# Moving the conditioning of a hybrid decoder step partly into its feed-forward stage, and changing three places of the hand-written order

## The chip, the core and the metric

The kernel is one program on one core of a Trainium2 chip. Its time is the device time in microseconds (us) of one execution of the program, inputs and outputs in the chip's memory. The core has a matrix engine (TensorE, PE in the profile), three engines for elementwise work (VectorE or DVE, ScalarE or ACT, GpSimd or POOL), and SyncE (SP), whose queue issues most of the DMA transfers here. PE works on operands in SBUF and writes to PSUM, from which VectorE and ScalarE read.

## What is computed

Two layers of a decoder, for 512 prompt positions and 8 samples of 4 positions, 544 columns in all, with 1024 features:

```
mod = (silu(c) @ w_ada + b_ada).reshape(B, 6, 1, D_MODEL)     # six sections
h = rmsnorm(x, norm1_g) * (1 + mod[:, 1]) + mod[:, 0]
z = h @ w_in
... four mixers on column ranges of z: pooling, retention, short convolution, RWKV-7
mixed = sum(sigmoid(gates) * (branches @ w_br)) @ w_out
x = x + mod[:, 2] * mixed
h2 = rmsnorm(x, norm2_g) * (1 + mod[:, 4]) + mod[:, 3]
up = causal_dwconv(h2 @ w_up);  act = silu(up[:D_FF]) * up[D_FF:]
x = x + mod[:, 5] * (act @ w_down)
```

After the second layer comes a final norm. The states of the mixers and of the convolution are outputs too. All matrices are float32.

So each of the six sections of the conditioning `mod` has a place at which it must be there: 0 and 1 at a layer's start, 2 at the residual after the mixers, 3 and 4 at the second norm, and 5 at the residual of the down projection. Layer 1's sections depend on `c` alone and can be computed at any time before.

## The kernel before, in words

**Layout and weights.** Activations lie with features on the 128 partitions and the 544 columns along the free dimension, in two halves of 272 (`HS`). The large matrices are cut into "units" of eight 128 x 128 tiles (0.5 MB), 138 per layer, in the order in which they are used. `load_unit` (L100) brings a unit in through a buffer `raw` (three of them), ScalarE casts it to a high part (L109), VectorE (GpSimd for two units) subtracts to get a low part (L110). `mm3` (L125) then takes three matmuls per tile: high x high, high x low, low x high (L129, L130, L131). A unit's products with all 544 columns are thus 48 matmuls. `getw(l, u, ahead)` issues loads up to unit `u + ahead`. There are four buffers for a unit's high and low parts; `extra_pools` can give a unit other buffers, among them a large tile of the pool `T4` (14 tiles of 2176 floats per partition).

**Order.** PE's order is the order of the program text. The other engines and SP's queue are ordered by a planner when the program is built, which can place an instruction earlier than its place in the text. Side work is written as generators that `slot` (L154) advances, called after each `mm3`: a generator yields how many main matmuls must pass before its next step (`yield 30`); a negative number makes a step that needs no PE slot, `True` marks a "tiled" step, that is one with many small matmuls. A generator with a slack (`spawn(..., 60)`) waits for such a tiled step, or until it is 60 matmuls late while another generator is due, or 240 otherwise. `finish(e)` runs all remaining steps of a generator at once.

**Conditioning.** Sections 0 and 1 of layer 0 are computed at the start. `ada` (L216) computes other sections: eight slices of weights are loaded, one after the other (0.5 MB each for one section, 1 MB for two sections at once), each is multiplied in four PE column groups (L225), the result is copied (L231), transposed back (L235) and added to the bias. It pauses at the start of each section (`yield 60`), between slices (`yield 30 * ns`) and before the transposes (`yield 18`). Layer 0's sections 2 to 5 run as `ada0` with slack 60 beside the mixers, through the same `raw` buffers as the weights; `finish(ada0)` (in the layer's loop, after the last gate) ends them before the output projection. Layer 1's six sections run in pairs as `ada_next` beside layer 0's up projection, through `T4` tiles.

**Norms by halves.** `both_halves` (L311) runs a projection first for the columns of one half, then of the other; while the second half is projected, the first is normalised (`norm_half`, L292). The second half is normalised while the next projection runs on the first: four units at the start of layer 1 (`for i in range(4)`), and four units, the first two pairs (`up_pairs([0, 1], True)`), at the start of each feed-forward stage.

**RWKV.** `rwkv` (L383) prepares 32-step blocks, inverts a 32 x 32 triangular matrix for each block and head by a substitution on VectorE (`substitute`, L558 and L560), writes the inverses to memory (`scr2`) and reads them back block by block into a diagonal tile `XT`, which has to be zero elsewhere (L569). Then 16 chunks follow one another: per chunk a matmul L639, copies by ScalarE and VectorE (`g_out`, L601), a matmul L606 after `D_G` = 12 main matmuls, copies (`sa_of`, L610), after `D_S` = 12 more the matmuls L659 and L663, VectorE's update of the state (L671, L677), and after `D_P` = 18 the next chunk. At the same time the main stream runs the other mixers; the pooling branch (two units) ends each of them with a series of VectorE additions and scalings (L1133 to L1152).

**Feed-forward.** `up_pairs` and `down` alternate: ten pairs, `down(0)`, four pairs, `down(1)`, eight pairs, `down(2)`, `down(3)`. The results of two pairs share one `T4` tile (`acts`), which lives until the `down` that uses it is over.

Of the kernel before, what the change touches and what calls it, by code (L numbers as in the profile page):

```python
# [11 lines left out]
F32R = mybir.dt.float32r  # L12
# [31 lines left out]
def tile_hybrid_step(ctx: ExitStack, tc: tile.TileContext, io: dict):  # L44
    nc = tc.nc
    V, S, G, PE = nc.vector, nc.scalar, nc.gpsimd, nc.tensor
    L = io["wst"].shape[0]
# [50 lines left out]
    extra_pools = {}  # L98

# [116 lines left out]
    def ada(l, sec, ns, load):  # L216

        W = 256 * ns
        ps = PM()
        raws = [load(k) for k in range(ns)]  # L220
        yield 60
        for k in range(0, 8, ns):
            for i in range(ns):
                for n in range(4):
                    PE.matmul(ps[32 * n:32 * n + 32, 0:W], lhsT=sc[:, k + i, :], rhs=raws[k + i][:, W * n:W * n + W],  # L225
                              start=(k + i == 0), stop=(k + i == 7))
            if k + ns < 8:
                raws.extend(load(k + ns + i) for i in range(ns))
                yield 30 * ns
        sb = ZR(W)  # L230
        S.copy(sb, ps[:, 0:W])  # L231
        yield 18
        pt = PM()
        for q in range(2 * ns):
            PE.transpose(pt[:, q * 128:(q + 1) * 128], sb[:, q * 128:(q + 1) * 128], ident)  # L235
        V.tensor_tensor(
            out=mods[l][:, 8 * sec:8 * sec + 8 * ns, :].rearrange("p (n q) j -> p n q j", q=2 * ns),
            in0=pt[:, 0:W].rearrange("p (q n j) -> p n q j", q=2 * ns, n=4)[:, :, :, 0:9],
            in1=pars[l][:, P_BADA + 8 * sec:P_BADA + 8 * sec + 8 * ns].rearrange("p (n q) -> p n q", q=2 * ns).unsqueeze(3)
            .broadcast_to([128, 4, 2 * ns, 9]), op=ADD)  # L240
        scales(l, range(sec, sec + ns), slice(0, 8))

    def ada_load(l, sec, ns):
        def f(k):
            if ns == 1:
                t = wp.tile([128, 1024], F32, tag="raw", name=nm("raw"), bufs=3)
            else:
                t = T4(w=(2176,))[:, 0:2048]
            nc.sync.dma_start(t.rearrange("p (s n) -> p s n", s=ns), io["wada"][l, sec:sec + ns, k].rearrange("s p n -> p s n"))
            return t  # L250
        return f

    def ada_all(l, secs, ns):
        for q in secs[::ns]:
            yield from ada(l, q, ns, ada_load(l, q, ns))
# [127 lines left out]
    def rwkv(l, za, zb, M, yD):  # L383
# [157 lines left out]
        nc.sync.dma_start(X, io["xinit"])  # L541
        yield 24
# [24 lines left out]

        XT = T4(w=(17, 128))
        G.memset(XT, 0.0)  # L569
# [5 lines left out]
        yield 48  # L575
# [360 lines left out]
    for l in range(L):  # L936
# [61 lines left out]
        else:  # L998
            ws = [getw(l, u) for u in range(4)]
            for half in range(2):  # L1000
                for i in range(4):
                    evac_rw(i, unit(ws[i], 0, hops, half), half)
                finish(ng)
            nfirst = 4
# [7 lines left out]
        if l == 0:  # L1012
            ada0 = spawn(ada_all(0, range(2, 6), 1), -30, 60)
# [196 lines left out]
        def extra(i):  # L1210
            def f():
                if i < 2:
                    return (wop.tile([128, 1024], F32R, name=nm("woh")), wop.tile([128, 1024], F32R, name=nm("wol")))
                t = T4(F32R, w=(2176,))
                return t[:, 0:1024], t[:, 1024:2048]
            return f
        for i in range(4):
            extra_pools[(l, ui + 4 + i)] = extra(i)
# [24 lines left out]
        if l + 1 < L:  # L1243
            ada_next = spawn(ada_all(l + 1, range(6), 2), -60)
# [73 lines left out]
        up_pairs([0, 1], True)  # L1318
        up_pairs(range(2, 10))
# [8 lines left out]
        for i in range(4, FFN_PARTS[3][1] - FFN_PARTS[3][0]):  # L1328
            extra_pools[(l, ui + i)] = extra(2)
# [215 lines left out]
```

## Time and profile before

| | |
|---|---|
| median of 3 runs | 1988.12 us (1980.52, 1988.12, 1989.43) |
| the profiled execution | 1981.39 us, its span 1979.3 us |
| granted TensorE clock, mean | 0.991 |
| PE busy | 1908.6 us, 96% |
| VectorE, ScalarE, GpSimd busy | 1111.1, 822.2, 322.6 us |
| HBM read, written | 213.33 MB, 9.06 MB |

The profile's times are those of one execution, in us from its first instruction. A row of a group reads: line, engine, operation, output <- inputs, then the count and the durations; "idle before <- releaser" is what an engine waited for. A row of the waits reads: who <- for whom: total, times, longest. A row of the windows gives the stretch, its width, the busy time of PE, of the weight loads, of VectorE, ScalarE and GpSimd, each with the number of instructions, then the granted clock, the DMA engines' share and GB/s; where it is asked for one source line, only PE's columns stand. A row of the timeline reads: start, duration, engine, line, operation, shapes, count, and the idle time before it with its cause. A row of the DMA issues gives count, size and the median time to landing.

### The profile page before, as it was taken

The numbers are of one execution on the slowest core, as the hardware profiler recorded it, in microseconds if no ns is written. First come the engines' busy times: TensorE is split into PE (matmuls) and PEld (weight loads), VectorE is DVE, ScalarE is ACT, GpSimd is POOL, SyncE is SP. The second block draws the span as 40 slices with busy tenths as digits, with TensorE's granted clock in tenths as the row PEclk, the third lists the DMA queues.
The fourth block names the chain that finished last, engine by engine and source line by source line (L and its number), as shares of the span: only waits on it lengthen the run. The fifth ranks groups of instructions, "written<-read, shape, count | busy, mean of one in ns | idle before, by whom it ended". The sixth has DMA issues, their size and how long they took to land. (4 is left out here: it accounts for less than half of the span.)

```text
span 1979.3 us, 39216 instructions
## 1 busy us (share of the span) xinstructions
PE 1908.6 (96%) x16188; PEld 1831.9 (93%) x16188; DVE 1111.1 (56%) x2267; ACT 822.2 (42%) x1574; POOL 322.6 (16%) x627
## 2 busy tenths in 40 slices
PE   5999899999999999999999998999999999999997
PEld 4999889899988889999999998899999999999997
DVE  5476655643457454556664766555435666455565
ACT  4642333452345442435446432335424565243542
POOL 2120123213001110112202201232120022011210
PEclk9999999999989999999999999999999999999999
DMA  7334234433446752222332132134224132222231
GB/s 310 97 100 125 90 99 139 154 108 97 140 158 241 269 203 96 86 86 86 114 125 87 57 105 68 44 100 132 76 97 163 51 97 93 90 86 86 88 102 46
DMA packets 75555, 227.15 MB, mean 115 GB/s; under 512 B 20209, under 2 KB 23073, under 8 KB 73585
## 3 DMA queue, kind: packets, MB, share of 16 engines
q1 hardware_dynamic: 69872, 210.43, 31.7%
q0 software_dynamic: 3536, 11.53, 1.7%
q10 hardware_dynamic: 1968, 2.69, 0.5%
q8 instruction: 127, 2.08, 0.4%
q14 instruction: 52, 0.42, 0.1%
HBM read 213.33 MB, written 9.06 MB: 112 GB/s over the span
## 5 line engine op out<-in xcount | busy, mean ns | idle before, releaser
L129 PE MATMUL pd<-t,whi 128*128 128x272 f32 x4200 | 1235.9, 294 | 8.5 <-DVE zr L337 3.7
L131 PE MATMUL pd<-t,wlo 128*128 128x272 f32 x4200 | 1216.3, 290 | 0.0
L130 PE MATMUL pd<-t,whi 128*128 128x272 f32 x4200 | 1210.5, 288 | 0.9 <-DVE t L381 0.7
L129 PEld LDWEIGHTS pd<-t,whi 128*128 128x128 f32 x4200 | 792.8, 189 | 40.3 <-issue 26.7
L130 PEld LDWEIGHTS pd<-t,whi 128*128 128x128 f32 x4200 | 794.7, 189 | 2.7 <-DVE t L381 1.8
L131 PEld LDWEIGHTS pd<-t,wlo 128*128 128x128 f32 x4200 | 793.4, 189 | 0.0
L110 DVE TENSOR_TENSOR wlo<-raw,whi 128x1024 fp32r<-128x1024 f32 x262 | 325.1, 1241 | 294.7 <-ACT whi L109 293.1
L109 ACT CAST whi<-raw 128x1024 fp32r<-128x1024 f32 x264 | 276.8, 1050 | 401.8 <-PE pd L130 384.3
L1257 POOL COPY off<-zr 128x18 f32<-128x18 f32 x88 | 77.9, 886 | 556.6 <-ACT zr L1255 556.6
L333 DVE SCALAR_TENSOR_TENSOR t<-pd,mod,t 128x272 f32<-128x272 f32 (+1 forms) x160 | 76.9, 482 | 107.9 <-PE pd L131 107.6
L1092 DVE TENSOR_TENSOR zr<-pd,zr 128x272 f32<-128x272 f32 x96 | 41.1, 437 | 113.7 <-PE pd L131 113.0
L1255 ACT COPY zr<-pd 128x272 f32<-128x272 f32 (+2 forms) x264 | 72.6, 310 | 70.8 <-PE pd L131 70.8
L1107 ACT ACTIVATE zr<-pd 128x272 f32<-128x272 f32 x128 | 50.5, 394 | 112.3 <-PE pd L131 111.8
L1093 POOL TENSOR_TENSOR t<-t,zr 128x272 f32<-128x272 f32 x64 | 69.6, 1105 | 126.3 <-DVE zr L1092 118.8
L1022 DVE SCALAR_TENSOR_TENSOR zr<-zr,par,zr 128x560 f32<-128x560 f32 x92 | 73.7, 802 | 9.3 <-ACT zr L1021 9.3
L1021 ACT ACTIVATE zr<-zr,par 128x560 f32<-128x560 f32 x92 | 70.4, 765 | 17.8 <-DVE zr L1046 9.8
L380 ACT CAST t<-zr 128x544 fp32r<-128x544 f32 (+1 forms) x96 | 49.4, 530 | 65.7 <-DVE zr L1268 65.0
L1023 DVE SCALAR_TENSOR_TENSOR zr<-zr,par,zr 128x560 f32<-128x560 f32 x92 | 73.6, 801 | 2.9
L381 DVE TENSOR_TENSOR t<-zr,t 128x544 fp32r<-128x544 f32 (+1 forms) x96 | 54.4, 582 | 32.3 <-ACT t L380 31.9
L264 ACT ACTIVATE zr<-t 128x272 f32<-128x272 f32 (+1 forms) x72 | 31.9, 454 | 86.4 <-DVE t L333 55.1
L601 ACT COPY gs<-pm 32x64 f32<-32x64 f32 x68 | 13.7, 202 | 70.3 <-PE pm L639 68.2
L267 DVE TENSOR_TENSOR zr<-zr,zr 128x272 f32<-128x272 f32 (+1 forms) x63 | 29.9, 475 | 19.9 <-ACT zr L264 19.1
(281 smaller groups left out, 1700.7 us busy)
## 6 DMA issues: line engine op xcount, KB each, us to landing
raw<-in_wst SPq DMA_DIRECT2D x276, 512.0 KB, 3.4
t<-in_wada SPq DMA_DIRECT2D x32, 1024.0 KB, 9.8
raw<-in_wada SPq DMA_DIRECT2D x32, 512.0 KB, 3.5
zr<-in_rope POOLq DMA_DIRECT2D x16, 272.0 KB, 3.6
t<-in_xT SPq DMA_DIRECT2D x4, 544.0 KB, 6.4
zr<-zr ACTq DMA_DIRECT2D x32, 68.0 KB, 2.1
t<-in_xT SPq DMA_DIRECT2D x2, 1088.0 KB, 7.6
xs<-t SPq DMA_DIRECT2D x2, 1088.0 KB, 4.3
```

The costliest lines, as they stand in the source:

```text
L109: S.copy(hi, raw)
L110: (G if (l, u) in ((0, 1), (0, 2)) else V).tensor_tensor(out=lo, in0=raw, in1=hi, op=SUB)
L129: PE.matmul(ps, lhsT=a, rhs=xh, start=first, stop=False)
L130: PE.matmul(ps, lhsT=a, rhs=xl, start=False, stop=False)
L131: PE.matmul(ps, lhsT=b, rhs=xh, start=False, stop=last)
L333: V.scalar_tensor_tensor(out=x[:, c0:c0 + npc], in0=ps[:, :npc], scalar=gate[:, m, 0:1], in1=x[:, c0:c0 + npc], op0=MUL, op1=ADD)
L1021: S.activation(cv, u[:, 0:560], AF.Copy, scale=wcol(0))
L1022: V.scalar_tensor_tensor(out=cv, in0=u[:, 1:561], scalar=wcol(1), in1=cv, op0=MUL, op1=ADD)
L1023: V.scalar_tensor_tensor(out=cv, in0=u[:, 2:562], scalar=wcol(2), in1=cv, op0=MUL, op1=ADD)
L1093: (V if last else G).tensor_tensor(out=a[:, c0:c1], in0=a[:, c0:c1], in1=gs, op=ADD)
L1255: pad_evac(lambda o, i, sl: S.copy(o, i), u, ps, half, 2)
L1257: G.tensor_copy(off[:, 22 * s + j], u[:, 512:562].rearrange("p (x t) -> p x t", t=2)[:, 0:25:3, :])
```

## The change

- The tile `XT` is allocated and cleared before the substitution in the text, not after it, and the pause between its loads and the scan is 66 main matmuls instead of 48.
- `ada` is one generator over all slices of all its sections: `pair` slices per step, the next pair loaded when the present one has been multiplied, one pause `gap` per step, and the closing transposes of a section in the step after its last slice. Layer 0's sections 2 to 4 run as `ada0` beside the mixers (one slice per step, gap 24). Section 5 runs as `ada5` beside layer 0's up projection, two slices per step in `T4` tiles, gap 48. Layer 1's sections run as `ada_next` from `down(0)` on, two slices of 1 MB per step, gap 60.
- At the start of layer 1 six units instead of four run on the first half, at the start of each feed-forward stage three pairs instead of two; the fifth and sixth unit take a `T4` tile each. At layer 1's start the loads ahead are those of the six units alone (`getw(l, u, 0)`).

```diff
--- before.py
+++ after.py
@@ -96,6 +96,10 @@
 
     wloaded = {}
     extra_pools = {}
+
+    def extra_t4():
+        t = T4(F32R, w=(2176,))
+        return t[:, 0:1024], t[:, 1024:2048]
 
     def load_unit(l, u):
         raw = wp.tile([128, 1024], F32, tag="raw", name=nm("raw"), bufs=3)
@@ -213,46 +217,52 @@
         scales(0, (1,), slice(k, k + 1))
         yield
 
-    def ada(l, sec, ns, load):
+    def ada(l, secs, ns, pair, load, gap):
 
         W = 256 * ns
-        ps = PM()
-        raws = [load(k) for k in range(ns)]
-        yield 60
-        for k in range(0, 8, ns):
-            for i in range(ns):
+        steps = [(q, k) for q in secs[::ns] for k in range(8)]
+        nxt = [load(*x) for x in steps[:pair]]
+        yield gap
+        close = None
+        for i in range(0, len(steps), pair):
+            cur = nxt
+            sec, k0 = steps[i]
+            if k0 == 0:
+                ps = PM()
+            for k, raw in enumerate(cur, k0):
                 for n in range(4):
-                    PE.matmul(ps[32 * n:32 * n + 32, 0:W], lhsT=sc[:, k + i, :], rhs=raws[k + i][:, W * n:W * n + W],
-                              start=(k + i == 0), stop=(k + i == 7))
-            if k + ns < 8:
-                raws.extend(load(k + ns + i) for i in range(ns))
-                yield 30 * ns
-        sb = ZR(W)
-        S.copy(sb, ps[:, 0:W])
-        yield 18
-        pt = PM()
-        for q in range(2 * ns):
-            PE.transpose(pt[:, q * 128:(q + 1) * 128], sb[:, q * 128:(q + 1) * 128], ident)
-        V.tensor_tensor(
-            out=mods[l][:, 8 * sec:8 * sec + 8 * ns, :].rearrange("p (n q) j -> p n q j", q=2 * ns),
-            in0=pt[:, 0:W].rearrange("p (q n j) -> p n q j", q=2 * ns, n=4)[:, :, :, 0:9],
-            in1=pars[l][:, P_BADA + 8 * sec:P_BADA + 8 * sec + 8 * ns].rearrange("p (n q) -> p n q", q=2 * ns).unsqueeze(3)
-            .broadcast_to([128, 4, 2 * ns, 9]), op=ADD)
-        scales(l, range(sec, sec + ns), slice(0, 8))
-
-    def ada_load(l, sec, ns):
-        def f(k):
-            if ns == 1:
+                    PE.matmul(ps[32 * n:32 * n + 32, 0:W], lhsT=sc[:, k, :], rhs=raw[:, W * n:W * n + W],
+                              start=(k == 0), stop=(k == 7))
+            if close:
+                close()
+                close = None
+            nxt = [load(*x) for x in steps[i + pair:i + 2 * pair]]
+            if k0 + pair == 8:
+                sb = ZR(W)
+                S.copy(sb, ps[:, 0:W])
+
+                def close(sec=sec, sb=sb):
+                    pt = PM()
+                    for q in range(2 * ns):
+                        PE.transpose(pt[:, q * 128:(q + 1) * 128], sb[:, q * 128:(q + 1) * 128], ident)
+                    V.tensor_tensor(
+                        out=mods[l][:, 8 * sec:8 * sec + 8 * ns, :].rearrange("p (n q) j -> p n q j", q=2 * ns),
+                        in0=pt[:, 0:W].rearrange("p (q n j) -> p n q j", q=2 * ns, n=4)[:, :, :, 0:9],
+                        in1=pars[l][:, P_BADA + 8 * sec:P_BADA + 8 * sec + 8 * ns].rearrange("p (n q) -> p n q", q=2 * ns).unsqueeze(3)
+                        .broadcast_to([128, 4, 2 * ns, 9]), op=ADD)
+                    scales(l, range(sec, sec + ns), slice(0, 8))
+            yield gap
+        close()
+
+    def ada_load(l, ns, wide):
+        def f(sec, k):
+            if wide:
+                t = T4(w=(2176,))[:, 0:1024 * ns]
+            else:
                 t = wp.tile([128, 1024], F32, tag="raw", name=nm("raw"), bufs=3)
-            else:
-                t = T4(w=(2176,))[:, 0:2048]
             nc.sync.dma_start(t.rearrange("p (s n) -> p s n", s=ns), io["wada"][l, sec:sec + ns, k].rearrange("s p n -> p s n"))
             return t
         return f
-
-    def ada_all(l, secs, ns):
-        for q in secs[::ns]:
-            yield from ada(l, q, ns, ada_load(l, q, ns))
 
 
     def xk(xt, k):
@@ -539,6 +549,9 @@
         nc.sync.dma_start(Nb[0:64], scr1)
         nc.sync.dma_start(Nb[64:128], scr1)
         nc.sync.dma_start(X, io["xinit"])
+
+        XT = T4(w=(17, 128))
+        G.memset(XT, 0.0)
         yield 24
         psN = PM()
         for q in range(2):
@@ -564,15 +577,12 @@
                 yield -14
         for h in range(2):
             nc.sync.dma_start(scr2[:, :, h, :], X[64 * h:64 * h + 64])
-
-        XT = T4(w=(17, 128))
-        G.memset(XT, 0.0)
         for q in range(2):
             for p in range(2):
                 nc.sync.dma_start(
                     XT[g_rows(q, p), 0:16, b_rows(q, p)],
                     scr2[(2 * q + p) * 16:(2 * q + p) * 16 + 16].rearrange("c s h t -> (s h) c t"))
-        yield 48
+        yield 66
 
         def values(t0):
 
@@ -996,12 +1006,14 @@
                     evac_rw(i, ps0[half][i], half)
             nfirst = 3
         else:
-            ws = [getw(l, u) for u in range(4)]
+            for i in (4, 5):
+                extra_pools[(l, i)] = extra_t4
+            ws = [getw(l, u, 0) for u in range(6)]
             for half in range(2):
-                for i in range(4):
+                for i in range(6):
                     evac_rw(i, unit(ws[i], 0, hops, half), half)
                 finish(ng)
-            nfirst = 4
+            nfirst = 6
         for i in range(nfirst, 8):
             w = getw(l, i)
             for half in range(2):
@@ -1010,7 +1022,7 @@
         yD, yB = [], []
         rw = spawn(rwkv(l, za, zb, M, yD), -3)
         if l == 0:
-            ada0 = spawn(ada_all(0, range(2, 6), 1), -30, 60)
+            ada0 = spawn(ada(0, range(2, 5), 1, 1, ada_load(0, 1, False), 24), -30, 60)
 
 
         yC = T4(F32R)
@@ -1207,15 +1219,10 @@
         wctx = ExitStack()
         wop = wctx.enter_context(tc.tile_pool(name=f"wo{l}", bufs=1, reuse_waits="tile"))
 
-        def extra(i):
-            def f():
-                if i < 2:
-                    return (wop.tile([128, 1024], F32R, name=nm("woh")), wop.tile([128, 1024], F32R, name=nm("wol")))
-                t = T4(F32R, w=(2176,))
-                return t[:, 0:1024], t[:, 1024:2048]
-            return f
+        def extra():
+            return (wop.tile([128, 1024], F32R, name=nm("woh")), wop.tile([128, 1024], F32R, name=nm("wol")))
         for i in range(4):
-            extra_pools[(l, ui + 4 + i)] = extra(i)
+            extra_pools[(l, ui + 4 + i)] = extra if i < 2 else extra_t4
         xt = [T4(), T4()]
         for i in range(2):
             nc.sync.dma_start(xt[i], xsrc[:, 4 * i:4 * i + 4])
@@ -1241,7 +1248,7 @@
         hops = ops_of(hh)
 
         if l + 1 < L:
-            ada_next = spawn(ada_all(l + 1, range(6), 2), -60)
+            ada5 = spawn(ada(l, [5], 1, 2, ada_load(l, 1, True), 48), -60)
         upads = {}
         acts = {}
 
@@ -1315,8 +1322,13 @@
                 for half in range(2):
                     run(m, half)
 
-        up_pairs([0, 1], True)
-        up_pairs(range(2, 10))
+        for i in (4, 5):
+            extra_pools[(l, ui + i)] = extra_t4
+        up_pairs([0, 1, 2], True)
+        up_pairs(range(3, 10))
+        if l + 1 < L:
+            finish(ada5)
+            ada_next = spawn(ada(l + 1, range(6), 2, 2, ada_load(l + 1, 2, True), 60), -12)
         down(0)
         up_pairs(range(10, 14))
         down(1)
@@ -1326,7 +1338,7 @@
         if l + 1 < L:
             finish(ada_next)
         for i in range(4, FFN_PARTS[3][1] - FFN_PARTS[3][0]):
-            extra_pools[(l, ui + i)] = extra(2)
+            extra_pools[(l, ui + i)] = extra_t4
         if l + 1 < L:
             nxt = new_hh()
             ng = both_halves(
```

## The prediction

> **What bounds the kernel now.** I read the page's busy times first, then who TensorE (PE) waited for over the whole span, then single stretches of it.
>
> ```profile
> PE 1908.6 (96%) x16188; PEld 1831.9 (93%) x16188; DVE 1111.1 (56%) x2267; ACT 822.2 (42%) x1574; POOL 322.6 (16%) x627
> ```
> ```profile
> PE pm L606 <- DVE gs L601: 15.0, 9, 3.9
> ...
> PE pd L129 <- DVE zr L337: 5.8, 4, 2.9
> PE pm L225 <- DMA raw<-in_wada: 4.7, 3, 3.1
> ```
>
> PE is busy 1908.6 of 1979.3 us, so at most 70.7 us can be won without removing matmuls, and this change removes none. Of the waits (total, times, longest), the change can touch three: L606 (15.0 us, the RWKV scan waiting for small VectorE copies; L659 is the same kind, below), L225 (4.7 us, conditioning waiting for its weights) and L337 (5.8 us, PSUM freed late while a norm occupies VectorE). A wait may cost more than itself, because the granted clock falls behind it:
>
> ```profile
> 552.50:554.90 2.40, 2.40 (x12) 2.40 (x11) 1.28 (x2) 1.93 (x2) 0.00 (x0) 0.50 0.89 285
> 850.00:900.00 50.00, 50.00 (x401) 50.00 (x400) 29.72 (x58) 17.40 (x29) 5.96 (x16) 1.00 0.29 96
> 1231.80:1234.10 2.30, 0.00 (x0) 0.01 (x1) 2.17 (x5) 0.00 (x0) 0.62 (x2) 1.00 0.61 160
> 1234.20:1237.50 3.30, 3.30 (x14) 3.07 (x14) 2.76 (x7) 0.80 (x3) 0.00 (x0) 0.50 0.19 78
> ```
>
> The columns are width, then PE, weight load, VectorE, ScalarE, GpSimd busy, then the clock. Undisturbed, a matmul takes 50/401 = 0.125 us, so a 48-matmul weight unit takes 6.0 us. A pause of 2.30 us is followed by 3.3 us at clock 0.50, which costs half of that, about 1.7 us more.
>
> **Part 1, the end of layer 0's conditioning: a gain of 7.7 us.** PE's timeline where the mixers end:
>
> ```profile
> 541.08 1.50 PE L225 MATMUL pm<-raw,sc 128*32 128x256 f32 x24
> 545.64 2.31 PE L225 MATMUL pm<-raw,sc 128*32 128x256 f32 x16 [3.05 <-DMA raw<-in_wada]
> 548.13 1.08 PE L225 MATMUL pm<-raw,sc 128*32 128x256 f32 x8 [0.19 <-DMA raw<-in_wada]
> 550.64 1.08 PE L225 MATMUL pm<-raw,sc 128*32 128x256 f32 x8 [1.43 <-DMA raw<-in_wada]
> 552.21 0.69 PE L235 MATMUL pm<-cst,zr 128*128 128x128 f32 x2 [0.49 <-ACT zr L231]
> 552.55 0.57 PE L129 MATMUL pd<-t,whi 128*128 128x272 f32 x1
> ...
> 554.74 0.36 PE L129 MATMUL pd<-t,whi 128*128 128x272 f32 x1
> ```
>
> finish(ada0) runs what is left of section 5 with nothing between it: 552.55 - 541.08 = 11.47 us without a main matmul, then nine matmuls in 2.19 us instead of 1.13, so 1.1 us by the clock. How much was left is in the rows of line L225 by stretch:
>
> ```profile
> 100.00:225.00 125.00, 5.11 (x64) 1.26 (x64) 1.00 0.38 114
> 225.00:317.00 92.00, 5.11 (x64) 1.26 (x64) 0.96 0.31 99
> 317.00:495.00 178.00, 5.11 (x64) 1.26 (x64) 1.00 0.38 123
> 495.00:541.00 46.00, 0.64 (x8) 0.16 (x8) 1.00 0.40 139
> 541.00:553.00 12.00, 5.83 (x56) 1.48 (x56) 0.65 0.78 260
> 600.00:740.00 140.00, 23.08 (x192) 5.01 (x192) 1.00 0.62 234
> ```
>
> A weight slice is 8 matmul records, so sections 2, 3 and 4 (64 records each) were through by 495, with pauses, and seven slices of section 5 stood at the end. The changed generator has no section 5 here, 25 steps instead of 36, and its first wait is 24 matmuls instead of 60; steps still fall on the scan's tiled steps. It is over before 495, and finish(ada0) finds nothing. The seven slices and the close don't vanish: they go into the FFN. One inserted slice costs 5.11/8 = 0.64 us; seven are 4.5, the close 0.34 (552.21 to 552.55). Gain: 11.47 + 1.1 - 4.5 - 0.3 = 7.8 us, less some 0.1 for entering and leaving the stream: 7.7. The output projection's weights, which came late behind these loads on SP's queue, are then early; PE waited for none of them, so that gains nothing.
>
> **Part 2, the cleared tile: nothing.** GpSimd's rows of the clearing (L569) and VectorE's first substitution step:
>
> ```profile
> L569 POOL MEMSET t<- x2: 1913/1914/1915, 143.5 to 1134.8; 128x2176 f32 x2
> ```
> ```profile
> 162.95 0.19 DVE L558 TENSOR_TENSOR t<-t 128x31 f32<-128x31 f32 x1 [0.44 <-DMA t<-in_xinit]
> ```
>
> The planner orders GpSimd itself and has the clearing at 143.5, 19 us ahead of the substitution, whatever its place in the source. It lies ahead of every load into the tile already; no wait goes. Were it not hidden, it would cost its 1.91 us per layer.
>
> **Part 3, "yield 66" for 48: a gain of 4 us, the least certain term.** It moves the whole scan 18 matmuls (2.25 us) along the main stream, and that changes what it collides with. PE and VectorE where the pooling branch's first unit ends, and the scan's waits in 185 to 345 (layer 0) and 1180 to 1330 (layer 1):
>
> ```profile
> 228.44 0.61 PE L639 MATMUL pm<-z,t 128*128 128x128 f32 x4
> ...
> 234.42 0.66 PE L606 MATMUL pm<-gs,t 128*128 128x64 f32 x2 [3.88 <-DVE gs L601]
> ```
> ```profile
> 229.59 0.96 DVE L1133 TENSOR_TENSOR t<-t 128x678 f32<-128x678 f32 x1
> ...
> 234.05 0.23 DVE L601 COPY gs<-pm 32x64 f32<-32x64 f32 x1
> ```
> ```profile
> PE pm L606 <- DVE gs L601: 6.7, 3, 3.9
> PE pm L659 <- DVE z L610: 2.4, 1, 2.4
> ```
> ```profile
> PE pm L606 <- DVE gs L601: 8.3, 6, 3.9
> ...
> PE pm L659 <- DVE z L610: 1.1, 1, 1.1
> ```
>
> The pooling arithmetic is a burst of some 4.5 us on VectorE. The second copy of gs stands behind it, and L606 comes only 12 matmuls (1.5 us) after L639, so PE stops 3.88 us; the second pooling unit does it again (the rest of layer 0's 6.7, some 2.3 us at L606, and 2.4 at L659). Shifted by 18, the step at this place is the one before, L659, whose result is wanted 18 matmuls later: 0.75 us more cover. The first stop becomes about 3.1; of the second pair one falls mostly in the holes between VectorE's dependent adds (I allow 0.4) and one stays at 2.3. That is 5.8 instead of 8.6 us in layer 0 and 7.3 in layer 1 (3.9 and the 2.30 at 1231.80 at L606, 1.1 at L659): 4.3 us in both, of which I count 4.1. Half-clock windows I leave at two per layer, as the stops of 3.9 and 2.3 suggest. From above, the gain is bounded by all of L606 and L659 (6.7 + 2.4 + 8.3 + 1.1 = 18.5) and four windows of 1.7: 25 us. From below, one more such stop per layer costs 2 x (3.9 + 1.7) = 11 us. I take 4, nearer to nothing, since the burst itself stays. The scan's end also comes 2.25 us later, and retention behind it: hidden by the units between them, at most 2 x 2.25 us.
>
> **Part 4, the rest of conditioning in the FFN: a loss of 1 us.** Layer 1's 12 batches move from the first ten up-projection pairs to down(0) and after; their PE time (23.08 us above) is the same. Their 24 loads of 1 MB go past the up-projections' weight loads on SP's queue and in among those of down(0) to down(1); section 5's eight of 0.5 MB come before them. What changes is the buffers. The pool has 14 large tiles. In down(0) live xt 2, hh 4 and five of acts: 11. A pair of slices is two tiles, with the next pair loaded ahead: four. 15 are wanted, so one load of each pair waits on SP until PE has used the pair before; behind it on SP stand the weight loads, which ACT, VectorE and then PE need three units (18 us) later.
>
> ```profile
> t<-in_wada SPq DMA_DIRECT2D x32, 1024.0 KB, 9.8
> ```
>
> The next batch comes after 60 matmuls (7.5 us) and the batch's own 1.9: 9.4 us against a landing of 9.8 in the median, where up to six were issued together; with two the queue is shorter. I take 1 us over the six batches, between 0 and the slow case below. Section 5 ends 60 + 5 x 48 = 300 matmuls after the FFN's start, the ten pairs are 960: no stop.
>
> **Part 5, six units on the first half: a loss of 0.5 us.** PE where four units run on one half today:
>
> ```profile
> 603.80:640.00 36.20, 36.20 (x292) 31.77 (x290) 25.12 (x56) 22.64 (x47) 4.47 (x15) 1.00 0.59 218
> 1033.90:1072.00 38.10, 38.10 (x304) 38.02 (x303) 21.57 (x51) 25.96 (x54) 6.82 (x19) 1.00 0.31 112
> ```
>
> There is no idle to remove: the norm's second half arrives in time behind four units. L337's waits lie ahead of these stretches, in the projection before. Against it stand two more splits that may be started there, in each of three places, where a 1.24 us subtraction (L110) delays an evacuation: 0 to 3 x 2.5 us.
>
> **The sum.** 1981.4 (the profiled execution; span 1979.3) - 7.7 - 4.1 + 1.0 + 0.5 = 1971. That execution lies 6.7 us under the median 1988.12; two of the three runs are near 1989, one near 1980.5. The level of the next runs isn't given by the profile, so I add half of the difference: 1975.
>
> By the row at 1231.80 a stop of 2.3 us halves the clock. The Trainium skill ("TensorE: Matmul & The Clock Gate", "Why this matters for your kernels") says that only idle gaps above some 3 us do; this trace disagrees, and the sum by it is the third rival.
>
> **The rivals.**
> - *The shift gains nothing*: the burst meets another step at the same price. For it: a burst blocks VectorE wherever it falls. 1981.4 - 7.7 + 1.5 = 1975, with the offset 1979. Chance 0.27.
> - *The shift clears the bursts*: all of 25 us. Against it: three steps in 42 matmuls, 4.5 us of burst. 1981.4 - 7.7 - 25 + 1.5 + 3.4 = 1954. Chance 0.08.
> - *The shortened stops leave the clock alone*: four windows of 1.7 us fewer, 1968. Against it the same row at 1231.80. Chance 0.08. It is what the Trainium skill's clock page, named above, would make of stops near 2.3 us.
> - *Slower: the fifteenth tile.* If a load in down(0) takes the 9.8 us above and counts only from the batch's end, each of six batches is 9.8 - 7.5 = 2.3 us late and halves the clock (1.7): 6 x 4.0 = 24 us, 1975 + 23 = 1998. It decides from 2.2 us per batch on (13 us in all). For it: today up to six loads run ahead; against it: two land sooner than six. Chance 0.11.
> - *The conditioning is still unfinished when the mixers end*, so nothing is won: 1985. Against it: the counts by 495. Chance 0.04.
>
> The forecast has 0.42, its own range 1969 to 1980. The range 1964 to 1988 leaves out the bursts cleared and the fifteenth tile, 0.19. Half a per cent is 9.9 us, about what this kernel's runs can tell: below 1978.2 is faster. Three quarters of the forecast (0.32), a third of the first rival (0.09) and the two fast ones, shaded for the runs' spread, give 0.53; slower has most of the fifteenth tile, 0.08; 0.39 is left.
>
> **What would show it.** Right: no row of L225 waiting for in_wada near 541, no clock 0.50 there; the memset still near 143; the stop at 230 near 3.1 us and on L639 instead of L606; PE full behind 603 and 1033. Wrong: PE idle with L225 waiting for t<-in_wada between 720 and 780; L606 still waiting 3.9 us; new L337 waits above 2 us, or the weights' casts late in the FFN.

## The result, and the profile after

The changed kernel is slower: 1996.47 us (median of 9, 1989.44 to 1997.66) against 1987.28 (median of 9, 1980.52 to 1989.68). The ratio is 1.0045, with a 95% interval of 1.003 to 1.0061. The forecast was 1975, in a range of 1964 to 1988. The two profiled executions differ by more, 1996.74 against 1981.39, since that of before lies 5.9 us under its median and that of after at its median. Where a difference of two traces is given below, it goes by these.

Busy times after, and whom PE waited for over the whole span (total, times, longest):

```profile
PE 1921.5 (96%) x16188; PEld 1839.5 (92%) x16188; DVE 1108.5 (56%) x2267; ACT 823.6 (41%) x1575; POOL 321.7 (16%) x627
```
```profile
PE pm L616 <- DVE gs L611: 10.0, 7, 2.9
...
PE pm L649 <- DVE z L687: 7.2, 5, 3.0
PE pd L133 <- DVE zr L347: 6.3, 5, 2.9
PE pm L738 <- DVE zr L724: 5.4, 3, 2.7
```

(Line numbers moved: L129 is now L133, L225 L234, L337 L347; in the scan by 10, so that L606 is now L616, L639 L649, L677 L687, L714 L724 and L728 L738, and behind it by 12, L1194 is L1206.) PE's busy time grew by 12.9 us with the same 16188 instructions, while the span grew by 15.6: most of the loss is not idle time, the same instructions took longer. Two waits of the scan are new: the one at L649, which took the place of some of L606's, and the one at L738, the last matmuls of the scan.

Every one of the 13,248 main matmuls is in both traces, so their starts can be compared one by one, counted from the first:

```
main matmul   where                       before     after   after - before
   960        layer 0, before the scan    189.22    189.06      -0.2
  2496        layer 0, scan over          466.83    474.66      +7.8
  2880        before the mixers' end      515.79    523.38      +7.6
  3072        mixers over                 552.55    547.91      -4.6
  5376        up-projections over         870.86    872.37      +1.5
  6720        layer 1 begun              1046.18   1048.35      +2.2
  7680        layer 1, before the scan   1192.20   1193.76      +1.6
  8640        layer 1, scan over         1375.75   1390.47     +14.7
 13152        near the end               1955.09   1969.78     +14.7
```

The conditioning does what was forecast (-12.2 at the mixers' end, some of it given back in the feed-forward stage, called FFN below). The loss is in the two scans: +8.0 and +13.1 us.

**Conditioning.** The rows of line L234 (L225 before) by stretch, and all engines in the stretch where PE had waited for weights:

```profile
317.00:495.00 178.00, 4.08 (x40) 0.87 (x40) 0.97 0.35 111
495.00:541.00 46.00, 0.00 (x0) 0.00 (x0) 1.00 0.38 130
541.00:553.00 12.00, 0.00 (x0) 0.00 (x0) 1.00 0.38 123
```
```profile
541.00:553.00 12.00, 11.89 (x94) 11.60 (x93) 8.68 (x18) 6.70 (x11) 0.00 (x0) 1.00 0.38 123
```

Nothing of it runs between 495 and 553; PE is full in the last 12 us of this, at full clock.

**The scan's end, layer 0.** ScalarE and VectorE before, then ScalarE, VectorE and PE after:

```profile
347.24 0.43 ACT L610 COPY z<-pm 32x64 f32<-32x64 f32 x2 [1.23 <-PE pm L606]
348.29 1.05 ACT L109 CAST whi<-raw 128x1024 fp32r<-128x1024 f32 x1 [0.62 <-PE pd L130]
349.37 0.39 ACT L1185 COPY zr<-pd 128x272 f32<-128x272 f32 x1
349.83 2.52 ACTq L1194 DMA_DIRECT2D zr<-zr  x4
```
```profile
347.54 0.69 DVE L714 TENSOR_TENSOR zr<-z,cst 64x512 f32<-64x512 f32 x1 [1.04 <-ACT z L610]
348.26 0.46 DVE L610 COPY z<-pm 32x64 f32<-32x64 f32 x2
348.75 2.12 DVE L714 TENSOR_TENSOR zr<-z,cst 64x512 f32<-64x512 f32 x3
...
354.66 0.93 DVE L1195 TENSOR_TENSOR zr<-zr,zr 128x544 f32<-128x544 f32 x1
```
```profile
352.73 0.41 ACT L611 COPY gs<-pm 32x64 f32<-32x64 f32 x2 [3.58 <-PE pm L715]
...
354.72 2.52 ACTq L1206 DMA_DIRECT2D zr<-zr  x4
357.28 0.43 ACT L620 COPY z<-pm 32x64 f32<-32x64 f32 x2 [2.65 <-issue]
```
```profile
357.59 0.69 DVE L724 TENSOR_TENSOR zr<-z,cst 64x512 f32<-64x512 f32 x1 [2.11 <-ACT z L620]
...
358.80 0.68 DVE L724 TENSOR_TENSOR zr<-z,cst 64x512 f32<-64x512 f32 x1
360.31 0.73 DVE L1207 TENSOR_TENSOR zr<-zr,zr 128x544 f32<-128x544 f32 x1 [0.83 <-DMA zr<-zr]
362.25 0.69 DVE L724 TENSOR_TENSOR zr<-z,cst 64x512 f32<-64x512 f32 x1 [1.22 <-POOL zr L1208]
362.98 0.73 DVE L1209 TENSOR_TENSOR t<-zr,zr 128x544 f32<-128x544 f32 x1
363.62 0.68 DVE L724 TENSOR_TENSOR zr<-z,cst 64x512 f32<-64x512 f32 x1
```
```profile
359.20 1.40 PE L738 MATMUL pm<-zr,t 64*64 64x512 f32 x4
363.09 3.22 PE L738 MATMUL pm<-zr,t 64*64 64x512 f32 x4 [2.49 <-DVE zr L724]
```

Before, the scan's last copy of sa (L610, the result of `sa_of`, tile `z`) comes first, the masked products Zx (L714) follow it in one run, and only then ScalarE issues the four DMAs by which a retention unit exchanges rows for its rotary product (L1194). Moved 18 matmuls along, the copy meets this unit: on ScalarE it stands behind the four issues, which hold the queue for 2.52 us, and on VectorE the second half of Zx stands behind the rotary product (L1207), which waits 0.83 us for the exchange to land, and then waits another 1.22 us for GpSimd's product on the exchanged rows (L1208). PE stops 2.49 us, and 2.66 at the same place in layer 1.

**The clock.** Windows of after, with the columns of the prediction's:

```profile
336.20:339.61 3.41, 3.41 (x87) 3.15 (x85) 3.06 (x7) 1.26 (x2) 2.32 (x3) 1.00 0.17 23
339.61:343.02 3.41, 3.41 (x22) 2.58 (x21) 0.44 (x1) 0.27 (x1) 1.54 (x3) 0.50 0.94 325
```
```profile
360.00:363.40 3.40, 0.91 (x4) 0.19 (x2) 1.84 (x3) 0.39 (x1) 1.88 (x1) 1.00 0.00 0
363.41:366.82 3.41, 3.41 (x12) 0.48 (x10) 2.49 (x6) 0.00 (x0) 1.04 (x1) 0.51 0.02 7
366.82:370.23 3.41, 3.41 (x21) 2.98 (x14) 1.26 (x2) 1.71 (x3) 2.20 (x3) 0.50 0.64 214
```

Behind the stop at L738 two steps of 3.41 us run at half clock. Another one follows 336.20 to 339.61, where PE didn't idle at all: there the state matmuls (L669, L673) and 64 matmuls of 8 columns (L700, the products on the sample states) fill the step, with five main matmuls in it instead of 27. Added up over the trace's clock records between 200 and 400 and between 1180 and 1380 us, half clock lasts 13.6 us before and 44.4 after.

### The profile page after: what moved, and what is told of

Read it like the earlier page. It is cut to its first block, busy times and chain, and to the rows that moved or that the text cites. A ratio compares the mean times of both kernels' runs of the same rounds, so it can differ in the third digit from the quotient of the medians.

```text
span 1994.9 us, 39203 instructions
## 1 busy us (share of the span) xinstructions
PE 1921.5 (96%) x16188; PEld 1839.5 (92%) x16188; DVE 1108.5 (56%) x2267; ACT 823.6 (41%) x1575; POOL 321.7 (16%) x627
## 4 chain that ended last, share of the span: by engine, by line
PE 87%; DVE 6%; ACT 2%; DMA 2%; issue 1%; ACTq 0%; POOL 0%; DVEq 0%; SPq 0%; POOLq 0%
PE pd L133 26%; PE pd L135 26%; PE pd L134 25%; PE pm L234 2%; DVE wlo L114 1%; DMA raw<-in_wst 1%; ACT whi L113 1%; PE pm L649 1%; PE pm L669 1%; DVE t L391 1%; PE pm L496 0%; PE pm L673 0%; DMA t<-in_wada 0%; PE pm L503 0%; DVE zr L307 0%
## 5 line engine op out<-in xcount | busy, mean ns | idle before, releaser
L133 PE MATMUL pd<-t,whi 128*128 128x272 f32 x4104 | 1211.4, 295 | 8.4 <-DVE zr L347 3.7
L135 PE MATMUL pd<-t,wlo 128*128 128x272 f32 x4104 | 1190.8, 290 | 0.0
L134 PE MATMUL pd<-t,whi 128*128 128x272 f32 x4104 | 1185.5, 289 | 1.1 <-DVE t L391 0.7
L133 PEld LDWEIGHTS pd<-t,whi 128*128 128x128 f32 x4104 | 777.2, 189 | 42.4 <-issue 27.8
L134 PEld LDWEIGHTS pd<-t,whi 128*128 128x128 f32 x4104 | 779.2, 190 | 3.2 <-DVE t L391 2.1
L135 PEld LDWEIGHTS pd<-t,wlo 128*128 128x128 f32 x4104 | 777.9, 190 | 0.0
L114 DVE TENSOR_TENSOR wlo<-raw,whi 128x1024 fp32r<-128x1024 f32 x256 | 317.9, 1242 | 296.9 <-ACT whi L113 296.5
L113 ACT CAST whi<-raw 128x1024 fp32r<-128x1024 f32 x258 | 270.4, 1049 | 423.2 <-PE pd L134 411.0
L133 PE MATMUL pd<-t,t 128*128 128x272 f32 x224 | 64.6, 288 | 0.5 <-DVE zr L347 0.5
L135 PE MATMUL pd<-t,t 128*128 128x272 f32 x224 | 64.6, 288 | 0.0
```

The costliest lines, as they stand in the source:

```text
L113: S.copy(hi, raw)
L114: (G if (l, u) in ((0, 1), (0, 2)) else V).tensor_tensor(out=lo, in0=raw, in1=hi, op=SUB)
L133: PE.matmul(ps, lhsT=a, rhs=xh, start=first, stop=False)
L134: PE.matmul(ps, lhsT=a, rhs=xl, start=False, stop=False)
L135: PE.matmul(ps, lhsT=b, rhs=xh, start=False, stop=last)
```

## The experiments

The theory (S): the 18 matmuls are the loss. The rivals: the FFN's moved loads (F), or a displaced phase that any edit upstream would bring (P). The first four kernels take the change apart.

**The change with the old pause.**

```diff
-        yield 66
+        yield 48
```

> The changed kernel with one number put back: the pause between the inverses' loads and the scan is 48 main matmuls again, not 66. Theory S (the 18 matmuls are the loss): the scan's last step no longer falls on the retention's rotary exchange, the two waits of line L738 for VectorE (2.5 and 2.6 us) and most of the 31 us of added half clock go, and the kernel takes about 5 to 6 us less than the kernel before, near 1982 us. Rival P (the clock's windows fall otherwise because everything ahead of the scan is displaced, or the conditioning's slices sit differently in it): the half-clock windows stay, and the time stays near 1996 us. Rival F (the FFN part costs more than it gives): near 1990 us or above, with no half clock added in the scan.

Measured: 1979.58 us (6 runs), ratio to before 0.9968 (0.9952 to 0.9985). There is no wait at L738. The pause alone is worth 1996.47 - 1979.58 = 16.9 us (some 15 by the two ratios), and all else in the change is a gain of some 7.

**The kernel before with the new pause only.**

```diff
-        yield 48
+        yield 66
```

> The kernel before with one number changed: 66 instead of 48, nothing else. Theory S: slower by 12 to 20 us, near 2001 us, with L728 (the product of the scan's last step) waiting for VectorE some 2.5 us in both layers and more than 20 us of added half clock. Rival P: within 4 us of the kernel before.

Measured: 1999.75 us (4 runs), ratio 1.0068 (1.0045 to 1.009), 12.8 us more. The same two waits, in the trace of this kernel:

```profile
353.75 2.51 ACTq L1194 DMA_DIRECT2D zr<-zr  x4
356.30 0.43 ACT L610 COPY z<-pm 32x64 f32<-32x64 f32 x2 [2.63 <-issue]
```
```profile
362.30 3.22 PE L728 MATMUL pm<-zr,t 64*64 64x512 f32 x4 [2.67 <-DVE zr L714]
```

**The conditioning only**: of the diff, the new `ada` and `ada_load` and their three calls.

```diff
-            ada0 = spawn(ada_all(0, range(2, 6), 1), -30, 60)
+            ada0 = spawn(ada(0, range(2, 5), 1, 1, ada_load(0, 1, False), 24), -30, 60)
...
-            ada_next = spawn(ada_all(l + 1, range(6), 2), -60)
+            ada5 = spawn(ada(l, [5], 1, 2, ada_load(l, 1, True), 48), -60)
```

> The kernel before with the conditioning's part of the change alone (the generator without pauses, section 5 in the FFN, layer 1's sections from down(0) on); tile, pause and units as before. By the main matmuls' starts the two profiles differ by -12.2 us where the mixers end and +7.1 us in the FFN, so 5 us less: near 1982 us. My prediction's term was -7.7 + 1 = -6.7 us. Rival F: no gain, 1987 us.

Measured: 1979.07 us (6 runs), ratio 0.9964 (0.9951 to 0.9977): a gain of 7.8 against the 1986.91 of the kernel before beside it.

**The six units only**, without the conditioning, the pause and the clearing.

```diff
-            ws = [getw(l, u) for u in range(4)]
+            for i in (4, 5):
+                extra_pools[(l, i)] = extra_t4
+            ws = [getw(l, u, 0) for u in range(6)]
...
-        up_pairs([0, 1], True)
+        up_pairs([0, 1, 2], True)
```

> The kernel before with six units (three pairs) on a norm's first half, nothing else. The profiles differ by 0.7 us at layer 1's start and show one added stop of 1.0 us in the FFN's start: 0 to 2 us slower, 1987 to 1989 us. If the norm's second half had been a hidden limit: 2 us or more faster.

Measured: 1986.23 us (10 runs), ratio 0.9998 (0.9985 to 1.001): no effect that can be told. S stands; F and P fall, since the FFN's part is a gain by itself and edits upstream without the pause don't bring the loss.

What in the scan makes the loss? Theory R holds that ScalarE's queue does, O that VectorE's order does. The next four kernels go after this.

**The exchange issued by SyncE**, on the changed kernel.

```diff
-                    S.dma_start(qs[32 * blk:32 * blk + 32, :], qn[32 * (blk ^ 1):32 * (blk ^ 1) + 32, :])
+                    nc.sync.dma_start(qs[32 * blk:32 * blk + 32, :], qn[32 * (blk ^ 1):32 * (blk ^ 1) + 32, :])
```

> The changed kernel with one thing moved: the four rotary exchange DMAs of each q/k unit of retention are issued by SyncE instead of ScalarE. 18 matmuls of pause stay. In the changed kernel these four issues occupy ScalarE's queue for 2.52 us at 354.72, the scan's last sa copies (L620) stand behind them until 357.28, and L738 then stops PE for 2.49 us and runs in a half-clock window. On VectorE the two multiplies of the rotary unit (L1207, L1209) stand between the two halves of the masked products Zx (L724), and the first of them waits for the exchange to land. Theory R (ScalarE's queue is the cause): sa copies at about 354.8, the stop at L738 and the windows behind it gone in both layers: 1996.5 - 2 x (2.5 + 3.0) = 1985 us. Theory O (VectorE's order is the cause: Zx's second half stands behind L1207 whoever issues the exchange): sa copies early, but L738 still stops 2 to 2.5 us and its windows stay: 1994 to 1998 us.

Measured: 1985.49 us (10 runs), ratio to before 0.9995 (0.9981 to 1.0009): 11 us of the loss are gone. ScalarE, SyncE, VectorE and PE at the scan's end:

```profile
351.44 0.42 ACT L611 COPY gs<-pm 32x64 f32<-32x64 f32 x2 [3.58 <-PE pm L715]
...
353.36 0.43 ACT L620 COPY z<-pm 32x64 f32<-32x64 f32 x2
```
```profile
353.41 2.50 SPq L1206 DMA_DIRECT2D zr<-zr  x4
```
```profile
358.51 0.87 DVE L1207 TENSOR_TENSOR zr<-zr,zr 128x544 f32<-128x544 f32 x1
359.41 0.69 DVE L724 TENSOR_TENSOR zr<-z,cst 64x512 f32<-64x512 f32 x1
```
```profile
360.24 1.04 PE L738 MATMUL pm<-zr,t 64*64 64x512 f32 x2 [1.28 <-DVE zr L724]
```

Counted from the copy of gs (`g_out`) ahead of it (L611), sa's copy (L620) starts 1.9 us later instead of 4.6; the stop is 1.28 instead of 2.49 us (1.33 for 2.66 in layer 1), and one step at half clock follows instead of two. What is left is O's: Zx's second half still stands behind L1207. Both theories hold a part, R the larger one in the time. Of the 7.8 us between the two profiled executions (1988.98 against 1996.74), 5.9 lie at this place in the two layers: 2.5 of stop, and two steps at half clock fewer.

**The scan's end in its old place**, all else of the scan 18 matmuls later.

```diff
-            yield D_P
+            yield D_P if ch < 15 else D_P - 18
```

> The changed kernel with the pause after the last chunk's products (ch = 15) 18 matmuls shorter: the whole scan stays 18 matmuls later, only its last step (the sample chunk, from the L649-like matmul at L715 on) is where it would be with a pause of 48. VectorE's order at the end is then that of before: all four parts of Zx, then the rotary multiplies. Theory S-end (the loss of the longer pause arises at the scan's end): no stop at L738, half clock behind it gone, the stops near 232 and 245 and the window near 339.6 unchanged: 1996.5 - 11 = 1985.5 us. Rival S-all (the shift displaces the clock's windows through the whole scan, and the end is one place among others): less than 4 us better, 1993 to 1997. If all of the loss of about 17 us were at the end it would be 1980.

Measured: 1982.55 us (10 runs, 1975.31 to 1983.86), ratio 0.9978 (0.9965 to 0.9992). No wait at L738, no half clock there, and Zx in one run again behind its first part:

```profile
349.82 2.12 DVE L724 TENSOR_TENSOR zr<-z,cst 64x512 f32<-64x512 f32 x3
```

13.9 of the 16.9 us of loss hang on where the last step stands. The profiled run is the fastest of the ten and also lacks the half-clock step behind the 64 products: in layer 0 six main matmuls lie in the step with 62 of them, and in layer 1 a boundary between two steps (1309.63) cuts them. What that means is told below.

**The products apart from the state matmuls.**

```diff
             if ch == 14:
+                yield 12
                 psG0 = PM()
...
-            yield D_P
+            yield D_P if ch != 14 else D_P - 12
```

> The changed kernel with 12 matmuls of main stream (1.5 us) put between the state matmuls of chunk 14 (L669, L673) and the 64 small products on the sample states (L700), and the pause after them 12 shorter, so that all later steps keep their place. Theory D (the 3.7 us without a main matmul, 2.04 of them 64 products of 8 columns, lower the granted clock): no half-clock window at about 339 and 1326, 1.7 us less each: 1996.5 - 3.4 = 1993 us. Rival (the window there comes from elsewhere, by an accident of the clock's own grid): window stays, 1996 to 1997 us. The stop at L738 stays in both.

Measured: 1993.42 us (5 runs), ratio 1.0035 (1.0022 to 1.0048), in the median 3.1 less than the changed kernel, where theory D expected 3.4. The interval overlaps that of the changed kernel (1.003 to 1.0061), so the time alone doesn't show a gain; the clock does. The step with the 64 products and the next one:

```profile
337.61:341.02 3.41, 3.41 (x77) 3.27 (x76) 1.42 (x3) 1.04 (x2) 2.27 (x5) 1.00 0.86 305
341.02:344.43 3.41, 2.61 (x22) 2.42 (x21) 2.00 (x4) 1.04 (x5) 0.71 (x1) 1.00 0.53 163
```

With seven main matmuls in the step of the products, the clock stays at 1.00 behind it; in layer 1 no half clock follows the products either. The stop at L738 stays, as expected.

**The old pause, and the exchange on SyncE.** Both edits shown above, 48 for 66 and SyncE for ScalarE.

> The changed kernel with the pause of before (48) and the exchange DMAs issued by SyncE: a candidate. With 48 there is no stop at L738 to take away, so by both theories it is as with 48 alone, 1979.6 us; where ScalarE's 2.5 us of issuing delayed an evacuation elsewhere (eight units per kernel) up to 2 us less, where the exchange waits on SyncE behind weight loads that have no buffer yet, up to 5 us more: 1977 to 1985.

Measured: 1979.57 us (9 runs), ratio 0.9969 (0.9955 to 0.9983), the same as with 48 alone. So moving ScalarE's 2.5 us of issuing gained nothing at the other places; they cost where a copy that PE soon wants stands behind them.

**Half of the way.** If the order at the end is what costs, then a pause for which the order doesn't flip should be harmless, although it is later than 48.

```diff
-        yield 66
+        yield 57
```

> The changed kernel with a pause of 57, half of the way from 48 to 66. In the instruction order of this version ScalarE's copy of sa (L620) stands ahead of the four rotary exchange issues (L1206), and on VectorE the four parts of Zx (L724) follow one another with no rotary multiply between, both as with 48. Theory A (what costs is the order at the scan's end, which flips between 57 and 66): no stop at L738 and no half-clock step behind it, 1996.5 - 12 = about 1984 or, if the steps behind the 64 products also stay at full clock, 1980 us. Rival M (a later scan is worse in proportion: every step of delay costs): half of the 17 us, 1988 us, with part of a stop at L738.

Measured: 1977.32 us (4 runs, 1976.09 to 1978.13), ratio to before 0.9948 (0.9934 to 0.9962). It is better than theory A said and 11 us from M's 1988. It beats both kernels; against a pause of 48 (1979.58, interval 0.9952 to 0.9985) the intervals overlap. Why it lies below theory A isn't shown: PE's stops of over 0.4 us in its two scans add up to 21.1 us, against 19.4 with 48, and half clock lasts 10.2 us against 23.9, but that is one execution each. ScalarE and VectorE:

```profile
350.24 0.43 ACT L620 COPY z<-pm 32x64 f32<-32x64 f32 x2
350.70 0.39 ACT L1197 COPY zr<-pd 128x272 f32<-128x272 f32 x1
351.16 2.55 ACTq L1206 DMA_DIRECT2D zr<-zr  x4
```
```profile
352.00 2.84 DVE L724 TENSOR_TENSOR zr<-z,cst 64x512 f32<-64x512 f32 x4
```

**Both mends on the changed kernel**: the end in its old place and the products apart.

```diff
+                yield 12
                 psG0 = PM()
...
-            yield D_P
+            yield D_P if ch < 14 else D_P - (12 if ch == 14 else 18)
```

> The changed kernel with both of the edits that each took a part of the loss away: the last chunk's pause 18 shorter (the scan's end where it is with 48) and 12 matmuls of main stream ahead of the 64 small products. In ten traces so far the granted clock changes only on a grid of steps of 3.41 us whose phase differs from run to run; every step of full clock in which PE stood 1.8 us or more was followed by one at half clock (52 of 52), and steps that held the 64 products and at most 5 main matmuls were too. Theory G (that rule): no step behind the products and none at the end can fall to half clock, whatever the phase; what is left are the stops near 232 and 247 in layer 0 and their counterparts in layer 1: 1982.6 less the 1.7 us that the products cost in the runs whose grid holds them whole, 1979 to 1981 us, about as with a pause of 48. Rival: the two gains overlap and it stays at 1982 to 1983 us.

Measured: 1981.53 us (8 runs), ratio 0.9974 (0.9961 to 0.9986), half a microsecond above what G expected and as much below the rival. In the trace no half-clock step is left at either place, as G said; the gain over the end alone (1982.55) is not told from nothing. A pause of 66, mended, is thus no better than 48 (1979.58).

## Why the prediction was wrong

**The step that failed** is the last sentence of part 3: "The scan's end also comes 2.25 us later, and retention behind it: hidden by the units between them, at most 2 x 2.25 us." It counted the delay of the scan's end as if the work kept its order. But ScalarE's and VectorE's orders are written by a planner, and a shift of 2.25 us let the first unit of retention pass the scan's last copy on both engines. The cost was 2.5 us of stop per layer and, with the clock behind it, 5.2 us of idle time and 6.8 of half-clock loss in both layers (four steps of 3.41, each worth half): 12.0 together; moving the end back alone gave 13.9. Part 3 was forecast as a gain of 4.1 us; the pause measured as a loss of 16.9, which makes 21.0 of the 21.5 us between the forecast and the time. The profile of before held the clue for ScalarE: its 2.52 us of issuing lay 2.16 us behind the end of the copy (347.67 to 349.83), less than the shift of 2.25. For VectorE it did not: the rotary product lay 3.8 us behind the end of Zx (350.87 to 354.66), more than the shift, and passed all the same. By what reckoning the planner put it ahead isn't on record.

**"Half-clock windows I leave at two per layer"** failed too. The 64 products, which bring a step at half clock in after, stood in the trace of before as well (331.98 to 334.02) without it; with 66 both layers got one in this trace, 3.4 us in all, and keeping the products apart gave 3.1 in the median, with intervals that overlap. Whether the pause brings these two steps isn't shown. The stretch without a main matmul around the products is as long with 48 as with 66 (3.5 us in layer 0, up to 3.9 where half clock falls into it, and 2.9 in layer 1); what differs is where a boundary of the clock's steps cuts it. In the four traces with 66 that leave the products whole, six of eight places were followed by half clock, in the six with 48 or 57 none of twelve. The account of the pause on the changed kernel: PE's stops of over 0.4 us in the two scans are 26.1 us with 66 and 19.4 with 48, half clock 44.4 and 23.9 us. 6.7 + 20.5/2 = 17 us, of 17.7 between these two executions. The six more steps at half clock are the four behind L738 and the two behind the products; the other seven are as many as with 48.

**Part 3's own term** had the place right and came to almost nothing. The stops at the pooling bursts became 5.9 us in layer 0, forecast 5.8, and 7.0 in layer 1, forecast 5.8:

```profile
234.58 0.80 PE L649 MATMUL pm<-z,t 128*128 128x128 f32 x4 [2.44 <-DVE z L687]
243.44 0.46 PE L649 MATMUL pm<-z,t 128*128 128x128 f32 x2 [0.64 <-DVE z L687]
248.27 0.66 PE L616 MATMUL pm<-gs,t 128*128 128x64 f32 x2 [2.86 <-DVE gs L611]
```

The first moved from L606 to the step before, as forecast, and is 2.44 for 3.1. But smaller stops at L616 appeared later in the scan (1.25 and 0.52 in layer 0; 1.50, 0.51 and 0.51 in layer 1, where before has 0.53, and 0.59 and 0.53), which takes back 2.6 of the 3.0 us gained at the bursts. The lower bound named for this part, one more such stop per layer, 2 x (3.9 + 1.7) = 11 us, is near what happened, but at a place that the prediction had called hidden; the range stopped at 1988, above it only the fifteenth tile was priced.

**Part 1** was right: 12.2 us gone where the mixers end and 0.8 in the matmuls behind it, which before ran at half clock, 13.0 in all; forecast 12.6 less 0.1. In the FFN 7.1 came back: 5.4 for the slices and the close (forecast 4.8; all eight slices of section 5 moved, seven were counted), the rest are two stops (1.04 and 0.60, below). With part 4 the forecast was 6.7 net, and the conditioning alone measured 7.8.

**Part 2** was right. The clearing stood at 143.5 before and stands earlier now:

```profile
L554 POOL MEMSET t<- x2: 1912/1912/1912, 118.9 to 1114.2; 128x2176 f32 x2
```

It was not timed alone, but the change with the old pause, which has it in the new place, takes as long as the conditioning alone, which has it in the old one (1979.58 and 1979.07 us).

**Parts 4 and 5** were small, as forecast. PE's stops in the FFN and at layer 1's start after:

```profile
650.09 0.39 PE L133 MATMUL pd<-t,whi 128*128 128x272 f32 x1 [1.04 <-ACT zr L1262]
813.20 1.06 PE L234 MATMUL pm<-t,sc 128*32 128x512 f32 x8 [0.60 <-DMA t<-in_wada]
1038.77 0.73 PE L285 MATMUL pm<-zr,cst 128*128 128x272 f32 x2 [1.19 <-DVE zr L277]
```

The conditioning's weights came late once, by 0.60 us (forecast 1 us in all), so the rival of the fifteenth tile falls: it needed 2.2 us per batch. The last row belongs to the six units: timed alone they have it too (1.09 us). The first is in neither the six units alone nor the conditioning alone, only where both stand. With it the two are about 2 us where 0.5 was forecast for the six units; timed alone, the six units changed nothing (0.9985 to 1.001).

**The rivals.** The shift neither gained nothing nor cleared the bursts, and the conditioning was finished. The slower rival had the right sign for another reason. None of them was that the order itself would change.

## The clock's steps, which I had not expected

In twelve traces (all named here) the granted clock changes only on a grid of 3.41 us. Its phase is one for a whole execution and differs from one trace to the next. Between 180 and 1900 us there are 5949 grid steps at full clock:

```
in the step                                     steps   next one at half clock
PE idle for 1.8 us or more                         60           60
PE idle for 1.5 to 1.8 us                          26            3
PE idle for less, under 60 of the 64 products    5854            6
60 or more of the 64 products, 0 to 5 main          5            5
60 or more of the 64 products, 6 to 12 main         4            1
```

The six of the third row held 0.9 to 1.4 us of idle time and at most four main matmuls. So it is not the length of a stop that decides, but how much of it falls into one step. The 2.30 us stop of the prediction is followed by half clock: all of it lay in one step (1230.72 to 1234.13). In the same execution the stop of 2.32 us ahead of 245.21 was cut by a boundary, and the clock stayed:

```profile
240.85:244.27 3.42, 2.04 (x17) 1.82 (x15) 2.71 (x5) 1.31 (x5) 1.50 (x2) 1.00 0.13 43
244.27:247.68 3.41, 2.33 (x20) 2.07 (x20) 3.08 (x6) 0.80 (x3) 0.00 (x0) 1.00 0.44 153
```

The stop of 2.87 us ahead of layer 1 (L337 at 1025.35) is followed by half clock before; after, the same stop (2.86 us, L347 at 1026.85) lies across a boundary at 1025.69 and goes free. Small matmuls count as little work here: a step without any idle time, but with 64 products of 8 columns and at most five main matmuls, is followed by half clock like an idle one. In the kernel before the same products lay across a boundary, and the clock stayed:

```profile
329.60:333.01 3.41, 3.41 (x66) 3.15 (x65) 1.39 (x5) 0.50 (x3) 0.81 (x2) 1.00 0.00 0
333.02:336.43 3.41, 3.41 (x57) 2.98 (x56) 0.00 (x0) 0.87 (x2) 0.21 (x1) 1.00 0.56 132
```

That the executions of the kernel before spread over 8.6 to 12 us in each batch may be this phase; it was not tested. In the three batches timed beside the experiments (17, 25 and 13 executions) those with a lower mean granted clock took longer, with a correlation of -0.5 in each, which fits. The Trainium skill ("TensorE: Matmul & The Clock Gate", "Part 1: The HAM clock gate") tells of a free-running window of about 3.4 us, with a phase that varies by run, and these traces agree. Its rule in "Why this matters for your kernels", that only idle gaps above some 3 us do harm, they don't bear out: 1.8 us within one step are enough here, 60 times out of 60.

Another thing: the four exchange DMAs held the queue of the engine that issued them for 2.5 us, on ScalarE (2.52 at 354.72) as on SyncE (2.50 at 353.41). Moving them from one to the other made the changed kernel 11 us faster, and the one with a pause of 48 not at all: what counts is what stands behind them.

## What to carry to other kernels

When a chain of small steps is shifted against a stream, list what stands next to its first and last step on every engine with a written or planned order, and how far away: a neighbour not much farther than the shift can change places (here 2.16 and 3.8 us for a shift of 2.25), and an instruction that waits for a DMA, or issues several, is then ahead of what PE needs. The planned order is known once the program is built: compare it before and after. Price a stop by the clock too, by how much of it can fall into one 3.41 us step, and keep large matmuls between blocks of small ones. A change made of several parts is timed part by part: here one number (57 instead of 66) turns a loss of 9 us into a gain of 10.
